# Building the one-hot gate rows of a product-key expert layer: two gated rows from one VectorE instruction in place of one from VectorE and one from GpSimd

## Chip, cores and metric

One Trainium2 chip, one of its cores. The metric is the device time in microseconds (us) of one execution of the whole program; lower is better. The engines that matter are PE (TensorE, the matmuls), DVE (VectorE), ACT (ScalarE), POOL (GpSimd) and SP (SyncE, which issues the DMAs).

## What is computed

Two blocks of a network on 256 tokens of 2048 channels in float32. The first holds a gated MLP and a stick-breaking attention, the second an mLSTM and convolution mixer and, at its end, a layer of product-key experts. Only the last is touched. Its core in the reference, cut:

```
q = (xt @ wq).reshape(-1, PEER_HEADS, 2, PEER_HALF)
s = jnp.einsum('thpc,hpnc->thpn', q, keys)
sv, si = lax.top_k(s, PEER_TOPK)                     # 16 best of 128 first keys, and of 128 second keys
...
eid = jnp.take_along_axis(cid, top_j, axis=-1)       # first key * 128 + second key: one of 16384 experts
gate = jax.nn.softmax(top_s, axis=-1)
act = jax.nn.gelu(jnp.einsum('thkd,td->thk', ue, xt))
return jnp.einsum('thk,thkd->td', gate * act, ve)
```

Each token has 8 heads with 16 experts each, so 128 pairs of keys, each with a gate.

## The kernel before

Nothing is gathered. All 16384 experts' input rows are multiplied with all tokens (the "up" loop over `u`, 32 chunks of 512 experts), the result goes through a GELU and to DRAM (`Ad`), is later multiplied with a dense matrix of gates `Gd` (zero where a token did not choose the expert), and goes into the second product with the experts' output rows.

**The matmuls.** `gemm` computes one 512-wide chunk of outputs from float32 weights that come as a stream of 1 MB tiles. Each tile is used in two halves. For a half, ACT rounds the raw weights to `wh` (line 191, from `Stream._high`), DVE makes the remainder `wl` (line 128, from `Stream._low`), and PE runs 12 matmuls of 512 columns (lines 315 to 317, in turn `wh`, `wl`, `wh`). ACT is up to six halves ahead and DVE up to five.

**The background.** Other work is written as Python generators. Between two halves `gemm` calls `bg.step()`, which takes each live generator to its next `yield`. This fixes the order of instructions on every engine when the program is built. A chunk has 8 such steps, one for each half.

**The gate matrix.** `gates_all` is such a generator and runs beside the first 16 or so chunks of the up loop. It first transposes, per token, the numbers of the first keys, of the second keys and the gates, so that tokens lie along the free axis and the 128 choices of a token on the partitions (tile `f5`: `i0`, `i1`, `gh`, `gl`). `gh` is the gate rounded to float32r and `gl` the remainder. Then, for every pair of tokens, `build` writes one-hot rows:

```
V.tensor_scalar(a[:, j, 0], C("iota"), i0[:, t:t + 1], gh[:, t:t + 1],
                op0=ALU.is_equal, op1=ALU.mult)                             # line 1181, DVE
nc.gpsimd.tensor_scalar(c[:, j], C("iota"), i1[:, t:t + 1], None, op0=ALU.is_equal)   # line 1183
nc.gpsimd.tensor_scalar(a[:, j, 1], C("iota"), i0[:, t:t + 1], gl[:, t:t + 1],
                        op0=ALU.is_equal, op1=ALU.mult)                     # line 1184, POOL
```

A matmul of `c` with both rows of `a` (line 1199, 256 columns, one for each token) gives, for one token, the 128 by 128 gates in two parts. ACT copies the one part out of PSUM, DVE adds the other (line 1204), and after 8 tokens SP sends the rows to `Gd`.

256 tokens make 128 pairs, so 128 steps, one for each half of a weight tile. A step's program: 12 weight matmuls, then two matmuls of line 1199 for pair k, then `build` for pair k+2, then the copy and the add of pair k. `a` and `c` each have three buffers in rotation (slots 0, 1, 4 and 2, 3, 5 of the tiles `e`), so the rows of pair k+3 can be written once the matmuls of pair k are done.

Of the kernel before, what the change touches and what calls it, by code (L numbers as in the profile page):

```python
# [9 lines left out]
ALU = mybir.AluOpType  # L10

P = 128
# [72 lines left out]


class Stream:
    """Weight tiles in the order of use: loaded ahead, split by halves into two float32r parts."""

    RAW, HI, LO = 3, 6, 5  # L90

# [50 lines left out]
                self._high()  # L142

    def next(self):
        """The next half, the ones before it being done with."""
        self.done = self.used
        self.ahead()
        return self.take()
# [18 lines left out]
def _block(ctx, tc, A, out):  # L167
    nc = tc.nc
# [6 lines left out]
    table = [None]  # L175
# [6 lines left out]
            table[0] = SETS[func]  # L182

    def act(out, in_, func, **kw):
        """An activation; exp and ln share the table set that holds both."""
        if func not in (AF.Copy, AF.Identity, AF.Abs, AF.Square):
            if func in SETS:
                table_for(func)
            else:
                table[0] = func  # L190
        S.activation(out, in_, func, **kw)  # L191
# [6 lines left out]
        return sb.tile([P] + shape, dt, name=nm(tag), tag=tag, bufs=bufs)  # L198

    def ft(i, shape, dt=F32):  # L200
        """A view of one of the 4 KB slots."""
        return _view(sb.tile([P, 1024], dt, name=nm(f"f{i}"), tag=f"f{i}"), shape)

    def et(i, shape, dt=F32):
        """A view of one of the 2 KB slots."""
        return _view(sb.tile([P, 512], dt, name=nm(f"e{i}"), tag=f"e{i}"), shape)

    turn = {}
# [13 lines left out]
    def ps():  # L222
        return pp.tile([P, 512], F32, name=nm("ms"), tag="ms", bufs=4)

# [1 line left out]
    order = []  # L226

    def add_w(name, n, kgs):
# [37 lines left out]
    st = Stream(nc, sb, order, act)  # L266
    bg = Background()

# [1 line left out]
    nc.scalar.preload_act_table_set("gelu_apprx_tanh_and_others")  # L270
    table[0] = AF.Gelu_apprx_tanh
    pv = tile("pv", [PW])
# [15 lines left out]
    def C(n):  # L288
        return con[:, CO[n][0]:CO[n][0] + CO[n][1]]
# [9 lines left out]

    ident = C("ident")  # L300

# [1 line left out]
    def gemm(xh, xl, kmap, evac, need={}, by_token=False):  # L303
        """One 512-wide chunk of outputs; kmap: first k tile of each stream tile;
        need: background work to end before a stream tile is used; by_token: the
        first 128 tokens end, and leave, ahead of the others."""
        acc = [pp.tile([P, 512], F32, name=nm("acc"), tag=f"acc{t}", bufs=2) for t in range(2)]
        last = len(kmap) - 1

        def mm(t, kk, wh, wl, k, first, fin):  # L310
            a = xh[:, kk, t * P:(t + 1) * P]
            b = xl[:, kk, t * P:(t + 1) * P]
            wa = wh[:, k * 512:(k + 1) * 512]
            wb = wl[:, k * 512:(k + 1) * 512]
            E.matmul(acc[t], a, wa, start=first, stop=False)  # L315
            E.matmul(acc[t], a, wb, start=False, stop=False)  # L316
            E.matmul(acc[t], b, wa, start=False, stop=fin)  # L317

        for i, k0 in enumerate(kmap):
            if by_token and i == last - 1:  # L320
                ks = [k0, k0 + 2, kmap[last], kmap[last] + 2]
                st.done = st.used
                st.ahead()
                w = [st.take() for _ in ks]
                for t in range(2):
                    for j, kk in enumerate(ks):
                        for k in range(2):
                            mm(t, kk + k, *w[j], k, i == 0 and j == 0 and k == 0, j == 3 and k == 1)
                        if t and j < 2:
                            st.release()  # L330
                        if j < 3:
                            bg.step()
                    evac(acc, t)
                    bg.step()
                return
            bg.finish(*need.get(i, []))
            for half in range(2):
                if half:
                    bg.step()
                wh, wl = st.next()  # L340
                for t in range(2):
                    for k in range(2):
                        first = i == 0 and half == 0 and k == 0
                        fin = i == last and half == 1 and k == 1
                        kk = k0 + 2 * half + k
                        mm(t, kk, wh, wl, k, first, fin)
            if i < last:
                bg.step()
        r = evac(acc)
        bg.step()  # L350
        return r
# [1 line left out]
    FULL = [0, 4, 8, 12]  # L353

    def transpose4(src, dst):
        """src(t, j) -> [128 tok, 128 ch] for 4 channel blocks; calls dst(pair, psum [128, 2, 256])."""
        for pr in range(2):
            p = ps()
            for jj in range(2):
                for t in range(2):  # L360
                    E.transpose(p[:, jj * T + t * P:jj * T + (t + 1) * P], src(t, pr * 2 + jj), ident)  # L361
            dst(pr, p)
# [10 lines left out]
        return tile(tag, [w], bufs=bufs)  # L373

    def rstd_of(dst, var, eps):
        """(var + eps) ** -0.5, a square root and a Newton step."""
        w = var.shape[-1]
        y = sm("rsy", 8, bufs=2)[:, :w]
        a = sm("rsa", 8, bufs=2)[:, :w]
        if eps is not None:  # L380
            ve = sm("rsv", 8, bufs=2)[:, :w]
            V.tensor_scalar(ve, var, eps, None, op0=ALU.add)
        else:
            ve = var
        act(y, ve, AF.Sqrt)
        V.reciprocal(y, y)
        V.scalar_tensor_tensor(a, y, -0.5, y, op0=ALU.mult, op1=ALU.mult)
        V.tensor_tensor(a, a, ve, op=ALU.mult)
        V.scalar_tensor_tensor(dst, a, 1.5, y, op0=ALU.add, op1=ALU.mult)
# [19 lines left out]
        V.scalar_tensor_tensor(d, mean, -1.0, c, op0=ALU.mult, op1=ALU.mult)  # L409
        return d  # L410

    # ================ layer 0: gated MLP with spatial gating ================
    xh = tile("xs", [NKT, T], F32R, bufs=4)
    xl = tile("xs", [NKT, T], F32R, bufs=4)
    def xprep(i, before):
# [190 lines left out]
    for n in range(4):  # L606
        out_chunk(n, 7, fin1)

    # ================ layer 1: stick-breaking attention ================
    bg.finish(p1tasks[0])  # L610
    x1h, x1l = x1["h"], x1["l"]
    r1 = x1["rstd"]
# [42 lines left out]
        V.tensor_copy(osb[g][:, :, c0:c0 + P], o[:, :256].rearrange("p (t c) -> p t c", t=2))  # L655

    def staged(gens, gap=2):
        """Chains run one stage apart, with `gap` steps of other work between the stages."""
        live = []
        while gens or live:  # L660
            for a in list(live):
                try:
                    next(a)
                except StopIteration:
                    live.remove(a)
            if gens:
                a = gens.pop(0)
                next(a)
                live.append(a)
            for _ in range(gap):  # L670
                yield
# [39 lines left out]
        gemm(x1h, x1l, FULL, ev, need)  # L711
        first = False

# [1 line left out]
    fgb = tile("phaseA", [D])  # L715
    o_ = RV["fg"][0]
    nc.sync.dma_start(out=fgb, in_=A["rows"][:, o_:o_ + D].to_broadcast([P, D]))
# [14 lines left out]
    bg.drain()  # L732

    def affine_prep(c, d, gname, bname):
        """h_res*c+d in place, then transposed with gain and bias into two parts."""
        nh = tile("xs", [NKT, T], F32R, bufs=4)
        nl = tile("xs", [NKT, T], F32R, bufs=4)

# [43 lines left out]
        return nh, nl, need  # L782

    def residual_affine(gname, bname, alloc):
        """Gain and bias on the residual itself, in the token layout."""
        gb = alloc(0)
        for n in range(4):
            g = bcast(gname, n * 512, 512, gb[:, 0:512])
# [18 lines left out]
    rstd_of(c_, ve, None)  # L807
    x2h, x2l, prep2 = affine_prep(c_, neg_prod(mean, c_), "lig", "lib")

    # ================ mLSTM and convolution mixer ================  # L810
    G5 = {}
    one = C("one")

# [223 lines left out]
        else:  # L1037
            gemm(x2h, x2l, FULL, ev)

# [1 line left out]
    st6 = new_stats(4, "st4")  # L1041
    bg.finish(*[yt5[k] for k in (("o", 0), ("o", 1), ("cB", 0))])
    for n in range(4):
# [17 lines left out]
    q7t = tile("xs", [4, 1024], bufs=4)  # L1061
    x3h, x3l, prep3 = affine_prep(*ln_scales(st6), "l1g", "l1b")

    # ================ product-key experts ================
    keysT = tile("phaseA", [16, P])
    nc.sync.dma_start(out=keysT, in_=A["keysT"])
    Gd = dr.tile([P, T, P], F32, name="Gd")
# [16 lines left out]
                yield  # L1084

    def route(n, q, before):
        """Top 16 of the products of keys for two heads; q: [128 tok, 2, 512]."""
        yield from wait(before)
        qT = ft(2, [4, T])

# [54 lines left out]
    def gates_all():  # L1145
# [27 lines left out]
        yield  # L1173

        def build(t0):
            """One-hot rows of two tokens: gates (two parts) by first key, ones by second key."""
            a = et(rot("oha", (0, 1, 4)), [2, 2, P], F32R)
            c = et(rot("ohb", (2, 3, 5)), [2, P], F32R)
            for j in range(2):
                t = t0 + j  # L1180
                V.tensor_scalar(a[:, j, 0], C("iota"), i0[:, t:t + 1], gh[:, t:t + 1],  # L1181
                                op0=ALU.is_equal, op1=ALU.mult)
                nc.gpsimd.tensor_scalar(c[:, j], C("iota"), i1[:, t:t + 1], None, op0=ALU.is_equal)  # L1183
                nc.gpsimd.tensor_scalar(a[:, j, 1], C("iota"), i0[:, t:t + 1], gl[:, t:t + 1],  # L1184
                                        op0=ALU.is_equal, op1=ALU.mult)
            return a, c

        ready = [build(0)]
# [70 lines left out]

    NP_ = NU // 2  # L1260
    def final(t):
        """Layernorm 2 of one tile of tokens, and out."""
        mv = sm("mv9", 2)
        V.bn_aggr(mv, st9[:, t])
        c = sm("cc", 1)
# [46 lines left out]


def _gate_rows(a):
    """16 rows of gates at partitions 0-7 and 32-39."""
    o = np.zeros((P,) + a.shape[1:], a.dtype)
    o[0:8], o[32:40] = a[:8], a[8:]
    return o
# [69 lines left out]
```

## Time and profile before

| | us |
|---|---|
| median of 3 runs | 3409.7 (3409.08 to 3410.12) |
| the profiled execution: span from first to last instruction | 3406.2 |
| PE busy in it | 3317.5 |
| DVE busy | 2067.0 |
| ACT busy | 1507.0 |
| POOL busy | 485.7 |
| POOL instructions of lines 1183 and 1184: first start, last start | 2054.2, 2529.2 |

The page gives the span of the profiled execution and no other time of it. The median of the runs is 3.5 us above that span. Busy times are those of one engine over the whole span; engines work beside one another, so they do not add up to it. POOL works almost only in one stretch of the program, between 2054 and 2530 us.

### The profile page before, as it was taken

The numbers are of one execution on the slowest core, as the hardware profiler recorded it, in microseconds if no ns is written. First come the engines' busy times: TensorE is split into PE (matmuls) and PEld (weight loads), VectorE is DVE, ScalarE is ACT, GpSimd is POOL, SyncE is SP. The second block draws the span as 40 slices with busy tenths as digits, with TensorE's granted clock in tenths as the row PEclk, the third lists the DMA queues.
The fourth block names the chain that finished last, engine by engine and source line by source line (L and its number), as shares of the span: only waits on it lengthen the run. The fifth ranks groups of instructions, "written<-read, shape, count | busy, mean of one in ns | idle before, by whom it ended". The sixth has DMA issues, their size and how long they took to land.

```text
span 3406.2 us, 39023 instructions
## 1 busy us (share of the span) xinstructions
PE 3317.5 (97%) x14722; PEld 2663.5 (78%) x14722; DVE 2067.0 (61%) x2966; ACT 1507.0 (44%) x1781; POOL 485.7 (14%) x522
## 2 busy tenths in 40 slices
PE   8999999999999999999999999888899999999998
PEld 6888888888888878888878887666678888888886
DVE  6565555565555566555579886555554666666666
ACT  5444444444444544444354444443344444444443
POOL 0000000000000000000000008999970000000001
PEclk9999999999999999999999999999999999999999
DMA  7565555545554445545555656555666666666664
GB/s 260 206 209 175 184 185 179 181 165 180 173 173 161 171 151 201 176 148 198 174 190 206 210 192 218 195 187 197 201 225 235 233 218 222 232 227 233 221 211 148
DMA packets 134348, 668.58 MB, mean 196 GB/s; under 512 B 12177, under 2 KB 45073, under 8 KB 62609
## 3 DMA queue, kind: packets, MB, share of 16 engines
q1 hardware_dynamic: 134160, 666.10, 56.7%
q8 instruction: 116, 1.90, 0.2%
q14 instruction: 72, 0.58, 0.0%
HBM read 630.40 MB, written 35.65 MB: 196 GB/s over the span
## 4 chain that ended last, share of the span: by engine, by line
PE 84%; POOL 14%; DVE 1%; ACT 0%; issue 0%; DMA 0%; SPq 0%; DVEq 0%; POOLq 0%
PE acc L315 27%; PE acc L316 26%; PE acc L317 26%; POOL e L1183 8%; POOL e L1184 6%; PE ms L1236 1%; PE ms L361 1%; PE ms L515 0%; DVE res L1272 0%; PE ms L1099 0%; PE ms L642 0%; PE ms L631 0%; DVE wl L128 0%; PE ms L751 0%; DMA raw<-in_aw_v_dram 0%
## 5 line engine op out<-in xcount | busy, mean ns | idle before, releaser
L128 DVE TENSOR_TENSOR wl<-raw,wh 128x1024 fp32r<-128x1024 f32 x1106 | 1343.9, 1221 | 669.4 <-PE acc L316 552.5
L191 ACT ACTIVATE wh<-raw 128x1024 fp32r<-128x1024 f32 x1106 | 1168.0, 1059 | 1198.5 <-PE acc L317 1136.3
L315 PE MATMUL acc<-wh,xs 128*128 128x512 f32 x4160 | 1662.0, 400 | 13.4 <-ACT wh L191 9.0
L316 PE MATMUL acc<-wl,xs 128*128 128x512 f32 x4160 | 1646.5, 396 | 0.5 <-DVE wl L128 0.5
L317 PE MATMUL acc<-wh,xs 128*128 128x512 f32 x4160 | 1645.9, 396 | 0.0
L315 PEld LDWEIGHTS acc<-wh,xs 128*128 128x128 f32 x4160 | 783.2, 188 | 194.2 <-ACT wh L191 9.0
L317 PEld LDWEIGHTS acc<-wh,xs 128*128 128x128 f32 x4160 | 782.6, 188 | 189.8 <-DVE xs L766 0.4
L316 PEld LDWEIGHTS acc<-wl,xs 128*128 128x128 f32 x4160 | 783.3, 188 | 178.0 <-DVE wl L128 1.0
L1183 POOL TENSOR_SCALAR e<-con,f 128x128 fp32r<-128x128 f32 x256 | 273.7, 1069 | 2053.7 <-ACT f L191 2053.7
L1184 POOL TENSOR_SCALAR e<-con,f 128x128 fp32r<-128x128 f32 x256 | 208.6, 815 | 0.0
L191 ACT ACTIVATE f<-ms 128x256 f32<-128x256 f32 (+3 forms) x153 | 62.7, 418 | 291.5 <-PE ms L1199 264.6
L1204 DVE TENSOR_TENSOR f<-ms,f 128x256 f32<-128x256 f32 x128 | 54.3, 424 | 198.1 <-ACT f L191 198.1
L1275 POOL TENSOR_TENSOR res<-res,xs 128x512 f32<-128x512 f32 x6 | 9.7, 1645 | 861.6 <-DVE res L1272 861.6
L1199 PE MATMUL ms<-e,e 128*128 128x256 f32 x256 | 82.7, 328 | 48.4 <-POOL e L1184 48.4
L1199 PEld LDWEIGHTS ms<-e,e 128*128 128x128 f32 x256 | 47.8, 187 | 92.9 <-POOL e L1184 86.5
L368 DVE TENSOR_TENSOR xs<-ms,xs 128x512 fp32r<-128x512 f32 x76 | 52.0, 690 | 110.1 <-ACT xs L191 110.1
L315 PE MATMUL acc<-wh,f 128*128 128x512 f32 x256 | 102.2, 399 | 0.0
L191 ACT ACTIVATE xs<-ms 128x512 fp32r<-128x512 f32 x76 | 44.8, 597 | 128.9 <-PE ms L1236 121.4
L316 PE MATMUL acc<-wl,f 128*128 128x512 f32 x256 | 101.2, 395 | 0.0
L317 PE MATMUL acc<-wh,f 128*128 128x512 f32 x256 | 101.2, 395 | 0.0
L1287 DVE TENSOR_TENSOR res<-res,acc 128x512 f32<-128x512 f32 x120 | 79.7, 683 | 35.1 <-PE acc L317 35.1
L1181 DVE TENSOR_SCALAR e<-con,f 128x128 fp32r<-128x128 f32 x256 | 83.4, 365 | 0.0
(213 smaller groups left out, 1355.5 us busy)
## 6 DMA issues: line engine op xcount, KB each, us to landing
raw<-in_pu_dram SPq DMA_DIRECT2D x128, 1024.0 KB, 4.9
raw<-in_pv_dram SPq DMA_DIRECT2D x128, 1024.0 KB, 4.8
raw<-in_bwi_dram SPq DMA_DIRECT2D x64, 1024.0 KB, 4.7
raw<-in_w_dram SPq DMA_DIRECT2D x56, 1024.0 KB, 4.7
raw<-in_aw_u_dram SPq DMA_DIRECT2D x32, 1024.0 KB, 4.7
raw<-in_aw_z_dram SPq DMA_DIRECT2D x32, 1024.0 KB, 4.8
raw<-in_awo_dram SPq DMA_DIRECT2D x32, 1024.0 KB, 4.7
raw<-in_aw_v_dram SPq DMA_DIRECT2D x31, 1024.0 KB, 4.8
```

The source lines that it names most:

```text
L128: self.nc.vector.tensor_tensor(l, raw[:, j * 1024:(j + 1) * 1024], self.hi[q].bitcast(F32), op=ALU.subtract)
L191: S.activation(out, in_, func, **kw)
L315: E.matmul(acc[t], a, wa, start=first, stop=False)
L316: E.matmul(acc[t], a, wb, start=False, stop=False)
L317: E.matmul(acc[t], b, wa, start=False, stop=fin)
L368: V.tensor_tensor(xl[:, k0 + 2 * pr:k0 + 2 * pr + 2, :], p.rearrange("p (k t) -> p k t", k=2), hv.bitcast(F32), op=ALU.subtract)
L1181: V.tensor_scalar(a[:, j, 0], C("iota"), i0[:, t:t + 1], gh[:, t:t + 1], op0=ALU.is_equal, op1=ALU.mult)
L1183: nc.gpsimd.tensor_scalar(c[:, j], C("iota"), i1[:, t:t + 1], None, op0=ALU.is_equal)
L1184: nc.gpsimd.tensor_scalar(a[:, j, 1], C("iota"), i0[:, t:t + 1], gl[:, t:t + 1], op0=ALU.is_equal, op1=ALU.mult)
L1199: E.matmul(p[:, j], c[:, j], a[:, j], start=True, stop=True)
L1204: V.tensor_tensor(d, p[:, :, 1], d, op=ALU.add)
L1287: V.tensor_tensor(d, d, acc[t], op=ALU.add)
```

## The change

`build` makes both gated rows of a token in one DVE instruction: a scalar_tensor_tensor that compares `iota`, repeated for two rows, with the first key, and multiplies with the two gates `gh` and `gl`, which lie side by side in `f5` (planes 2 and 3) and are each repeated along the row. POOL keeps the plain one-hot of the second key. Only docstrings and comment lines differ elsewhere; one line fewer in `build` moves later line numbers up by one (1199 is 1198 in the changed kernel, 1204 is 1203, and POOL's 1183 is 1184).

```diff
             for j in range(2):
                 t = t0 + j
-                V.tensor_scalar(a[:, j, 0], C("iota"), i0[:, t:t + 1], gh[:, t:t + 1],
-                                op0=ALU.is_equal, op1=ALU.mult)
+                V.scalar_tensor_tensor(a[:, j], C("iota")[:, None, :].to_broadcast([P, 2, P]), i0[:, t:t + 1],
+                                       f5[:, 2:4, t:t + 1].to_broadcast([P, 2, P]),
+                                       op0=ALU.is_equal, op1=ALU.mult)
                 nc.gpsimd.tensor_scalar(c[:, j], C("iota"), i1[:, t:t + 1], None, op0=ALU.is_equal)
-                nc.gpsimd.tensor_scalar(a[:, j, 1], C("iota"), i0[:, t:t + 1], gl[:, t:t + 1],
-                                        op0=ALU.is_equal, op1=ALU.mult)
             return a, c
```

How the instructions stand in their engines' queues. First POOL, at the rows of the third and fourth pair of tokens, before the change (line 1183 writes `c`, line 1184 the second row of `a`; each `e` with its two numbers is one such tile, `con` holds `iota`, `f` the transposed keys and gates; what an instruction waits for stands in brackets, DMAHW for a DMA, Pool and DVE for those engines):

```order
L1183 TENSOR_SCALAR e_760_14623<-con_71,f_748_14516 128x128 [waits DMAHW5_49,PE_49]
L1184 TENSOR_SCALAR e_759_14622<-con_71,f_748_14516 128x128 [waits DMAHW4_49]
L1183 TENSOR_SCALAR e_760_14623<-con_71,f_748_14516 128x128
L1184 TENSOR_SCALAR e_759_14622<-con_71,f_748_14516 128x128
L1183 TENSOR_SCALAR e_765_14654<-con_71,f_748_14516 128x128 [waits PE_49]
L1184 TENSOR_SCALAR e_764_14653<-con_71,f_748_14516 128x128 [waits DVE_49,Pool_49]
L1183 TENSOR_SCALAR e_765_14654<-con_71,f_748_14516 128x128
L1184 TENSOR_SCALAR e_764_14653<-con_71,f_748_14516 128x128
```

and the same place of the changed kernel, for the third to fifth pair:

```order
L1184 TENSOR_SCALAR e_760_14619<-con_71,f_748_14516 128x128 [waits DMAHW5_49,PE_49]
L1184 TENSOR_SCALAR e_760_14619<-con_71,f_748_14516 128x128
L1184 TENSOR_SCALAR e_765_14648<-con_71,f_748_14516 128x128 [waits PE_49]
L1184 TENSOR_SCALAR e_765_14648<-con_71,f_748_14516 128x128
L1184 TENSOR_SCALAR e_768_14677<-con_71,f_748_14516 128x128 [waits PE_49]
L1184 TENSOR_SCALAR e_768_14677<-con_71,f_748_14516 128x128
```

POOL has two instructions for a pair in place of four, the two that only compare; their wait on PE for the buffer stays, and the wait on DVE for the shared tile `a` is gone.

Then DVE, from the first add of line 1204 on, before the change:

```order
L1204 TENSOR_TENSOR f_757_14618<-ms_14619,f_757_14618 128x256 [waits Activation_49]
L128 TENSOR_TENSOR wl_14636<-raw_14502,wh_14596 128x1024 [waits DMAHW7_49]
L1181 TENSOR_SCALAR e_764_14653<-con_71,f_748_14516 128x128 [waits DVE_49,Pool_49]
L1181 TENSOR_SCALAR e_764_14653<-con_71,f_748_14516 128x128
L1204 TENSOR_TENSOR f_757_14618<-ms_14650,f_757_14618 128x256 [waits Activation_49]
L128 TENSOR_TENSOR wl_14665<-raw_14502,wh_14634 128x1024
```

and in the changed kernel:

```order
L1203 TENSOR_TENSOR f_757_14614<-ms_14615,f_757_14614 128x256 [waits Activation_49]
L128 TENSOR_TENSOR wl_14630<-raw_14502,wh_14592 128x1024 [waits DMAHW7_49]
L1181 SCALAR_TENSOR_TENSOR e_764_14647<-con_71,f_748_14516 128x256 [waits DVE_49]
L1181 SCALAR_TENSOR_TENSOR e_764_14647<-con_71,f_748_14516 128x256
L1203 TENSOR_TENSOR f_757_14614<-ms_14644,f_757_14614 128x256 [waits Activation_49]
L128 TENSOR_TENSOR wl_14657<-raw_14502,wh_14628 128x1024
```

The order on DVE is the same, with two instructions of 256 elements where there were two of 128, and no wait on POOL. On PE, ACT and SP no instruction is added, removed or moved.

## Rows read from the trace of the kernel before

**Rows 1.** The page's busy times of the engines.
```profile
PE 3317.5 (97%) x14722; PEld 2663.5 (78%) x14722; DVE 2067.0 (61%) x2966; ACT 1507.0 (44%) x1781; POOL 485.7 (14%) x522
```

**Rows 2.** The page's chain that ended last: by engine, then by line.
```profile
PE 84%; POOL 14%; DVE 1%; ACT 0%; issue 0%; DMA 0%; SPq 0%; DVEq 0%; POOLq 0%
PE acc L315 27%; PE acc L316 26%; PE acc L317 26%; POOL e L1183 8%; POOL e L1184 6%; PE ms L1236 1%; PE ms L361 1%; PE ms L515 0%; DVE res L1272 0%; PE ms L1099 0%; PE ms L642 0%; PE ms L631 0%; DVE wl L128 0%; PE ms L751 0%; DMA raw<-in_aw_v_dram 0%
```

**Rows 3.** Windows: length, PE, PEld, DVE, ACT, POOL busy (instructions), clock, DMA share, GB/s.
```profile
1854.00:1954.00 100.00, 100.00 (x447) 80.96 (x446) 86.07 (x222) 44.72 (x50) 0.00 (x0) 1.00 0.61 209
...
2254.00:2354.00 100.00, 89.08 (x380) 66.94 (x379) 57.45 (x109) 39.72 (x61) 100.00 (x109) 1.00 0.59 197
...
2530.00:2630.00 100.00, 99.98 (x438) 80.64 (x438) 47.86 (x44) 44.57 (x50) 0.00 (x0) 1.00 0.73 254
```

**Rows 4.** Waits between 2054 and 2530 us: total us, times, longest.
```profile
PEld ms L1199 <- POOL e L1184: 85.8, 119, 0.7
PE ms L1199 <- POOL e L1184: 48.0, 119, 0.4
```

**Rows 5.** Timeline: start, duration, engine, line; one step, and the last pair.
```profile
2200.94 0.39 PE L315 MATMUL acc<-wh,xs 128*128 128x512 f32 x1
...
2203.74 0.28 PE L1199 MATMUL ms<-e,e 128*128 128x256 f32 x1
...
2204.41 0.39 PE L1199 MATMUL ms<-e,e 128*128 128x256 f32 x1 [0.40 <-POOL e L1184]
...
2204.64 0.39 PE L315 MATMUL acc<-wh,xs 128*128 128x512 f32 x1
...
2529.34 0.28 PE L1199 MATMUL ms<-e,e 128*128 128x256 f32 x1
```

**Rows 6.** Timeline of PE, first and fifth pair of the stage.
```profile
2064.67 0.40 PE L1199 MATMUL ms<-e,e 128*128 128x256 f32 x2
...
2076.81 0.39 PE L1199 MATMUL ms<-e,e 128*128 128x256 f32 x2
```

**Rows 7.** Groups by form, 2054 to 2530 us: busy us, mean ns, idle before.
```profile
L1183 POOL TENSOR_SCALAR e<-con,f 128x128 fp32r<-128x128 f32 x256 | 273.7, 1069 | 2053.7 <-ACT f L191 2053.7
L1184 POOL TENSOR_SCALAR e<-con,f 128x128 fp32r<-128x128 f32 x256 | 208.6, 815 | 0.0
```

**Rows 8.** Groups by form of DVE, whole execution: nearest shapes to the new instruction.
```profile
L519 DVE SCALAR_TENSOR_TENSOR f<-ms,pv,f 128x256 f32<-128x256 f32 x32 | 14.0, 479 | 32.0 <-ACT f L191 18.8 <-PE ms L515 13.2
L1127 DVE TENSOR_TENSOR e<-e,f 128x256 f32<-128x256 f32 x32 | 13.6, 425 | 1.1
L419 DVE SCALAR_TENSOR_TENSOR xs<-xs,pv,xs 128x256 fp32r<-128x256 f32 x16 | 6.8, 478 | 8.2 <-ACT xs L191 8.2
```

**Rows 9.** Timeline of DVE, one step in which PE did not wait for POOL.
```profile
2071.59 0.42 DVE L1204 TENSOR_TENSOR f<-ms,f 128x256 f32<-128x256 f32 x1 [0.78 <-ACT f L191]
2071.93 1.22 DVE L128 TENSOR_TENSOR wl<-raw,wh 128x1024 fp32r<-128x1024 f32 x1
2073.07 0.60 DVE L1181 TENSOR_SCALAR e<-con,f 128x128 fp32r<-128x128 f32 x2
2074.63 0.42 DVE L1204 TENSOR_TENSOR f<-ms,f 128x256 f32<-128x256 f32 x1 [0.96 <-ACT f L191]
```

**Rows 10.** Lines 1183, 1184 (whole stage), 128 (2064 to 2530): ns minimum, median, maximum.
```profile
L1183 POOL TENSOR_SCALAR e<-con,f x256: 591/597/1646, 2054.2 to 2527.6; 128x128 fp32r<-128x128 f32 x128
L1184 POOL TENSOR_SCALAR e<-con,f x256: 787/792/1883, 2054.8 to 2529.2; 128x128 fp32r<-128x128 f32 x128
L128 DVE TENSOR_TENSOR wl<-raw,wh x127: 1215/1215/1349, 2066.2 to 2527.5; 128x1024 fp32r<-128x1024 f32 x127
```

**Rows 11.** Timeline, a POOL and a DVE instruction that meet, and POOL's next.
```profile
2068.73 0.79 POOL L1184 TENSOR_SCALAR e<-con,f 128x128 fp32r<-128x128 f32 x1
2069.51 1.21 POOL L1183 TENSOR_SCALAR e<-con,f 128x128 fp32r<-128x128 f32 x1
...
2068.90 1.35 DVE L128 TENSOR_TENSOR wl<-raw,wh 128x1024 fp32r<-128x1024 f32 x1
```

## The prediction

> **What bounds the kernel now.** I read the page first. PE is busy for 97% of the span and POOL for 14% [rows 1], which says "PE" and nothing of POOL. The chain of work that ended last says more: 84% of it is PE, but 14% lies on POOL, all on lines 1183 and 1184 [rows 2]. That is about 477 us in which the end of the program hung on GpSimd, as long as the stage in which the one-hot rows are built (2054 to 2530 us). So the windows come next: before and behind that stage PE is busy for 100 of 100 us, inside it for 89, while POOL is busy for 100 of 100 [rows 3]. The clock is 1.00 in all three, so no share of this is PE's clock. The waits inside the stage name the place: the weight load of line 1199, the one-hot matmul, waits 119 times for line 1184, 85.8 us together [rows 4].
>
> The timeline gives the size of one step. In a POOL-bound step the first weight matmul starts at 2200.94 and that of the next step at 2204.64, so 3.70 us; the pair of one-hot matmuls lies at 2203.74 and 2204.41, and the second stands until POOL's row is there [rows 5]. POOL itself needs for a pair of tokens two instructions of each line: 2 x 1069 + 2 x 815 ns = 3.77 us by the means of the stage [rows 7]; its instructions overlap by a few hundredths, hence 3.70. The stage also shows what PE needs by itself: at its start three pairs of rows are ready, and PE does not wait. Four such steps lie between 2064.67 and 2076.81, so 12.14 / 4 = 3.035 us each [rows 6]. The difference of 0.665 us, 128 steps long, is what can be had.
>
> **The change, part by part.**
>
> *POOL loses line 1184.* Per pair it keeps two comparisons. Undisturbed they take 597 ns (median), so 1.19 us a step; the stretched ones reach 1646 ns [rows 10]. The stretch comes from DVE: POOL's instruction that starts at 2069.51 takes 1.21 us and ends at 2070.72, 0.47 us after DVE's line 128 ended (2068.90 + 1.35 = 2070.25) [rows 11]. So POOL waits while DVE subtracts. One stretched and one free comparison make 1.65 + 0.60 = 2.25 us, below 3.035: POOL stops being the bound. The worst I can build is the rival below.
>
> *DVE gets a larger instruction.* The new one reads 256 elements twice from SBUF, with a scalar per partition, and writes float32r. The trace of before has no such instruction at this place, but the same kind and size elsewhere: 478 ns with both inputs in SBUF and a float32r output, 479 with one in PSUM; a plain two-input instruction of that size with repeated (broadcast) inputs takes 425 [rows 8]. I take 478, the row with the same operands; the ends are 425 and 479 before any waiting for POOL. Per step two of them take 0.96 us in place of the 0.60 that the pair takes in a step without PE waits [rows 9], so +0.36 us at most (back-to-back instructions overlap a little).
>
> *Is there room on DVE?* In such a step DVE starts the add of line 1204 at 2071.59, then line 128, then the pair until 2073.67, so 2.08 us; it stands idle for 0.96 until the next copy by ACT [rows 9]. With the change 2.08 + 0.36 = 2.44 of 3.035 us, so 0.6 us stay free. The cover is therefore this idle time; if it were gone, every further us on DVE would be a us on each step. Does a DVE busy for 2.6 us of 3.04 (86%: 0.42 + 1.22 + 0.96) hold PE up? Just ahead of the stage it is busy for 86 of 100 us with PE at 100 [rows 3]. POOL can also delay DVE: line 128 takes 1215 ns in the median and at most 1349 [rows 10], so one meeting cost up to 0.134 us; two a step make 0.27 and 2.71 us, still inside.
>
> *Moved waits.* DVE's instruction no longer waits for POOL, as both writers of tile `a` are now one. Behind it on DVE stands the add of line 1204, and behind that line 128, which is made up to five halves ahead of PE. The rows of a pair are written two steps before their matmul, and POOL may run up to three buffers ahead, so a late comparison or a late product has a step and more before PE sees it. ACT's copy is released by the matmul as before; ACT is at 40% in the stage [rows 3]. A GELU pair at a chunk's end (some 16 in the stage) may come ahead of that copy and make it late; it was so before as well, and DVE's idle time takes it.
>
> *DMA.* No transfer is added or moved, but the stage's transfers come in less time: 197 GB/s x 3.70 / 3.035 = 240 GB/s. Behind the stage 254 GB/s flow with PE at 99.98 of 100 us [rows 3]; I cost this at nothing.
>
> *The sum.* From the first one-hot matmul (2064.67) to that of the last pair (2529.34) [rows 5, 6] are 464.67 us for 127 steps. At 3.035 us they take 385.4, so 79.2 less; the last pair's own wait adds 0.67. Together 79.9 us. The waits count gives about the same: 119 times 0.665 is 79.1. Nothing else on the chain changes, since the stages around it keep PE at 100%. The profiled execution has a span of 3406.2 us and would have 3326.3; the median of the runs lies 3.5 us above that span, and I add the same. **3409.7 - 79.9 = 3329.8, say 3330 us.** Upwards, if a meeting on DVE at its largest (0.134 us) reached PE in a third of the steps, 43 x 0.134 = 6 us: 3336. Downwards nothing, as PE's own steps are the floor: 3329.
>
> **The rivals.**
>
> *POOL stays the bound, at a lower level.* The new instruction has two SBUF inputs, like line 128, and should stop POOL in the same way; line 1181 of before had one. If at every step the one comparison meets line 128 (1.65 us, the maximum) and the other the whole pair of new ones (0.60 + 0.96 = 1.56), POOL needs 3.20 us: 127 x 3.20 = 406.4 in place of 464.7, 58 to 59 us less with the last wait: 3351. For it: the stretch is in the trace at every step. Against it: DVE's 0.6 us of idle time a step let one comparison start undisturbed, and a POOL instruction that has started before DVE's runs on at its usual length (790 ns for the one of 2068.73, although DVE began 0.17 us later [rows 11]). Chance 0.10, spread over 3336 to 3351.
>
> *DVE becomes the bound, held by POOL for whole instructions.* If each comparison stopped DVE for its full 597 ns, DVE would need 2.44 + 1.19 = 3.63 us a step, 127 x 3.63 = 461.0: 4 us gained, 3405. With some of them falling into DVE's idle time or beside the add, which has one input in PSUM, the step is that of the two-input work and POOL alone, 1.22 + 0.96 + 1.19 = 3.37, 428 us: 3373. Against it: in the one meeting of this kind DVE was 0.13 us late, where the rest of POOL's instruction was 0.62 [rows 10, 11]. Chance 0.04. The Trainium skill has this as its rule (SBUF — State Buffer, section "Who interferes with whom"): a VectorE instruction with two SBUF inputs and a GpSimd one that reads SBUF exclude each other, the first to start keeps the shared port for the whole instruction, and the other stands still. By that rule the change would cost DVE what GpSimd gains. The trace agrees for POOL behind DVE, and not for DVE behind POOL.
>
> *Slower.* The same hold, but without the overlap of instructions that follow one another on DVE, which a stop in each of them would take away: then the busy times simply add up, 0.42 + 1.22 + 0.96 + 1.19 = 3.79 us a step, above the 3.70 of now. 127 x 3.79 = 481.3, 17 us more: 3426. It decides from the point at which DVE and POOL together need over 3.66 us (464.7 / 127), so from about 0.6 us of hold per comparison, four times the largest seen. Chance 0.02.
>
> *No gain, because another wait sits behind POOL's.* PE could find `wl` late, or the PSUM copy. Its steps at 3.035 us ran with DVE at 2.08 us of them, not with 2.44, so this is not shown. The loss would have no natural size; I put it anywhere between 3336 and 3410. Chance 0.02.
>
> **How the numbers follow.** The forecast, PE-bound steps throughout, has 0.82 and lies between 3329 and 3336. The range starts a us below that for the spread of the runs and takes in the nearer half of the first rival: 3328 to 3344. What a measurement of this kernel can tell from no change is about 0.2%, 7 us. Faster by more: the forecast, the first rival, most of the second and half of the fourth, 0.96. Within it: 0.02, the far ends of the second and fourth. Slower: 0.02.
>
> **What would show it.** In the profile after, PE should be at 99 or 100 of 100 us in the stage and the stage about 80 us shorter (some 390 us from the first to the last one-hot matmul); the wait of PE for POOL at the one-hot matmul gone; POOL's share of the chain gone; POOL busy for some 2 us a step; line 1181 at 256 elements and 0.48 us (up to 0.6 where it meets POOL); DVE idle for about 0.6 us a step before the add. I am wrong on POOL if its busy share in the stage is still 100 of 100; wrong on DVE if line 1181 takes 0.8 us or more, or line 128 well over 1.35, with PE waiting for DVE.

## Result and the profile after

| | before | after |
|---|---|---|
| median of 4 runs, us | 3409.85 (3409.08 to 3410.12) | 3328.47 (3327.70 to 3328.76) |
| span of the profiled execution, us | 3406.2 | 3327.0 |
| POOL busy, us | 485.7 | 162.9 |
| DVE busy, us | 2067.0 | 2107.4 |

The ratio of the runs is 0.9762, 95% interval 0.9748 to 0.9776: 81 us less. The forecast was 3330, the range 3328 to 3344. One of all the executions below, in the run with nothing on POOL, took 7159.67 us and is left out.

The page's busy times and its chain by engine, of the changed kernel, beside [rows 1, 2]:

```profile
PE 3286.7 (99%) x14722; PEld 2663.8 (80%) x14722; DVE 2107.4 (63%) x2966; ACT 1505.1 (45%) x1781; POOL 162.9 (5%) x266
...
PE 98%; DVE 1%; ACT 0%; DMA 0%; issue 0%; SPq 0%; DVEq 0%
```

POOL, 14% of the chain before, is gone from it. The windows of the changed kernel (length, then busy time of PE, PEld, DVE, ACT and POOL with instructions, clock, DMA share, GB/s), the first inside the stage and the second behind it, beside [rows 3]:

```profile
2254.00:2354.00 100.00, 100.00 (x464) 81.63 (x463) 80.63 (x132) 48.30 (x74) 39.02 (x66) 1.00 0.73 241
...
2450.00:2550.00 100.00, 100.00 (x440) 80.67 (x439) 48.06 (x45) 44.57 (x50) 0.00 (x0) 1.00 0.74 259
```

PE is at 100 of 100 us where it was at 89, and DMA moves 241 GB/s with no wait of PE. The waits of the stage (waiter, releaser: us in total, times, longest) have turned round: no engine waits for POOL, and POOL waits for PE, beside [rows 4]:

```profile
POOL e L1184 <- PE ms L1198: 235.3, 125, 5.8
ACT f L191 <- PE ms L1198: 184.6, 111, 1.7
DVE f L1203 <- ACT f L191: 76.9, 127, 1.9
```

The length of the stage is the first and the last start of the one-hot matmuls. In this view of the tile `e` stand the duration's minimum, median and maximum in ns, then the first and last start. First the kernel before:

```profile
L1199 PE MATMUL ms<-e,e x256: 275/281/388, 2064.7 to 2530.0; 128*128 128x256 f32 x128
```

and the changed one:

```profile
L1198 PE MATMUL ms<-e,e x256: 275/281/284, 2065.6 to 2450.9; 128*128 128x256 f32 x128
```

465.3 us became 385.3: 80.0 us are won here, and the longest matmul no longer holds a wait (388 ns before). The two spans differ by 79.2; the stage began 0.9 us later in this execution, in a part of the program that the change does not touch.

One step of the changed kernel on DVE, in the timeline (start, duration, what ended the idle time before), beside [rows 9], then POOL in the same step:

```profile
2202.92 0.42 DVE L1203 TENSOR_TENSOR f<-ms,f 128x256 f32<-128x256 f32 x1 [0.58 <-ACT f L191]
2203.27 1.32 DVE L128 TENSOR_TENSOR wl<-raw,wh 128x1024 fp32r<-128x1024 f32 x1
2204.51 0.87 DVE L1181 SCALAR_TENSOR_TENSOR e<-con,f 128x256 fp32r<-128x256 f32 x2
2205.96 0.42 DVE L1203 TENSOR_TENSOR f<-ms,f 128x256 f32<-128x256 f32 x1 [0.58 <-ACT f L191]
...
2202.57 1.18 POOL L1184 TENSOR_SCALAR e<-con,f 128x128 fp32r<-128x128 f32 x2 [1.85 <-PE ms L1198]
```

The step is 3.04 us (2202.92 to 2205.96). DVE stands idle for 0.58 of it, and POOL works for 1.18 and waits for 1.85. Both work beside PE with room to spare.

### The profile page after: what moved, and what is told of

Its sections match the earlier page's. It is cut to its first block, busy times and chain, and to the rows that moved or that the text cites. A ratio compares the mean times of both kernels' runs of the same rounds, so it can differ in the third digit from the quotient of the medians.

```text
span 3327.0 us, 38516 instructions
## 1 busy us (share of the span) xinstructions
PE 3286.7 (99%) x14722; PEld 2663.8 (80%) x14722; DVE 2107.4 (63%) x2966; ACT 1505.1 (45%) x1781; POOL 162.9 (5%) x266
## 4 chain that ended last, share of the span: by engine, by line
PE 98%; DVE 1%; ACT 0%; DMA 0%; issue 0%; SPq 0%; DVEq 0%
PE acc L315 31%; PE acc L316 31%; PE acc L317 31%; PE ms L1198 1%; PE ms L1235 1%; PE ms L361 1%; PE ms L515 0%; DVE res L1271 0%; PE ms L751 0%; PE ms L1099 0%; PE ms L642 0%; PE ms L631 0%; DVE wl L128 0%; DMA raw<-in_aw_v_dram 0%; ACT xs L191 0%; PE ms L898 0%
## 5 line engine op out<-in xcount | busy, mean ns | idle before, releaser
L1184 POOL TENSOR_SCALAR e<-con,f 128x128 fp32r<-128x128 f32 x256 | 153.0, 610 | 2289.9 <-ACT f L191 2054.6
L1181 DVE SCALAR_TENSOR_TENSOR e<-con,f 128x256 fp32r<-128x256 f32 x256 | 111.4, 474 | 0.0
L1286 DVE TENSOR_TENSOR res<-res,acc 128x512 f32<-128x512 f32 x120 | 79.7, 683 | 35.1 <-PE acc L317 35.1
L191 ACT ACTIVATE f<-acc 128x512 f32<-128x512 f32 x84 | 49.8, 598 | 38.0 <-PE acc L317 36.6
L539 DVE TENSOR_TENSOR res<-res,acc 128x512 f32<-128x512 f32 x64 | 43.7, 686 | 30.8 <-PE acc L317 30.8
L317 PEld LDWEIGHTS acc<-wh,f 128*128 128x128 f32 x256 | 48.1, 188 | 11.6
```

The costliest lines, as they stand in the source:

```text
L539: V.tensor_tensor(d, d, acc[t], op=ALU.add)
L1181: V.scalar_tensor_tensor(a[:, j], C("iota")[:, None, :].to_broadcast([P, 2, P]), i0[:, t:t + 1], f5[:, 2:4, t:t + 1].to_broadcast([P, 2, P ...
L1286: V.tensor_tensor(d, d, acc[t], op=ALU.add)
```

## Experiments

**Theory A**: a step takes the longest of three times, PE's 3.035 us, POOL's and DVE's. Before, POOL's was the longest (3.70); the change takes line 1184 from POOL, and PE's is left. **Theory B**: the gain came from the form of the new instruction (one for two), or from the end of the tile that two engines wrote.

### Both rows on DVE in the old form

```diff
-                V.scalar_tensor_tensor(a[:, j], ... i0[:, t:t + 1], ... op0=ALU.is_equal, op1=ALU.mult)
+                V.tensor_scalar(a[:, j, 0], C("iota"), i0[:, t:t + 1], gh[:, t:t + 1], ...)
+                V.tensor_scalar(a[:, j, 1], C("iota"), i0[:, t:t + 1], gl[:, t:t + 1], ...)
```

> Edit: both gated rows on DVE, but as two instructions of 128 elements per token (the old form), POOL keeps the plain row. Theory A (the step is the longest of PE's 3.035 us, POOL's time and DVE's time; the gain came from POOL's second line leaving POOL): POOL needs 1.19 us a step, DVE 0.34 + 1.24 + 4 x 0.30 to 0.34 = 2.8 to 2.95 us, both under 3.035, so the time is that of the changed kernel, 3328 to 3331 us, PE never waits for POOL. Theory B (the gain came from the fused instruction, which removes work on DVE or the shared writing of one tile by two engines): four instructions on DVE lose a part of it, 3345 us or more.

Measured: 3328.29 us, ratio to before 0.9759 (0.9743 to 0.9775), as the changed kernel. DVE's add now stands idle 0.34 us a step in place of 0.58:

```profile
2303.25 0.34 DVE L1183 TENSOR_SCALAR e<-con,f 128x128 fp32r<-128x128 f32 x1
2303.93 0.42 DVE L1204 TENSOR_TENSOR f<-ms,f 128x256 f32<-128x256 f32 x1 [0.34 <-ACT f L191]
```

So fusing the two rows saves DVE about 0.24 us a step, and the program nothing. The first half of theory B falls: without the new instruction the gain is the same.

### All gated rows on POOL

```diff
-                V.scalar_tensor_tensor(a[:, j], ... op0=ALU.is_equal, op1=ALU.mult)
+                nc.gpsimd.tensor_scalar(a[:, j, 0], C("iota"), i0[:, t:t + 1], gh[:, t:t + 1], ...)
+                nc.gpsimd.tensor_scalar(a[:, j, 1], C("iota"), i0[:, t:t + 1], gl[:, t:t + 1], ...)
```

> Edit: the opposite way, both gated rows on POOL, none on DVE. No tile is written by two engines any more. Theory A: POOL's step grows from 3.70 us by two instructions of 0.79 us to 5.28 us, so 127 x (5.28 - 3.035) = 285 us over the changed kernel, 3613 us (3600 to 3640). Theory B (two engines writing one tile was the cost): not slower than the kernel before, 3410 us or less.

Measured: 3583.44 us (one run), below the expected 3600 to 3640. No tile has two writers here, and the time is 173 us over before, which is not what theory B expects. The step is 5.05 us, not 5.28 as expected: POOL's timeline has the comparison that meets line 128 at 1.38 us where it was 1.57 in the kernel before, since it had started 0.30 us after line 128 (2302.33) and not 0.11:

```profile
2301.86 0.79 POOL L1183 TENSOR_SCALAR e<-con,f 128x128 fp32r<-128x128 f32 x1
2302.63 1.38 POOL L1185 TENSOR_SCALAR e<-con,f 128x128 fp32r<-128x128 f32 x1
2304.00 0.79 POOL L1181 TENSOR_SCALAR e<-con,f 128x128 fp32r<-128x128 f32 x1
```

### The row goes on being made on POOL, for nobody

```diff
+        scr = tile("scr", [2, P], F32R)
...
+                nc.gpsimd.tensor_scalar(scr[:, 0], C("iota"), i0[:, t:t + 1], gl[:, t:t + 1], ...)
```

> Edit: the changed kernel, and POOL still makes its old gated row of each token, into a scratch tile that nobody reads. Theory A: POOL's instructions are in order, so the plain row of the next token stands behind the useless one and POOL is the bound again: 3.70 us a step or, as the new DVE instruction stops POOL too, up to 3.70 + 0.96 = 4.66 us: 3413 to 3535 us. Theory B (what mattered is who waits for the row, not POOL's time): 3328 to 3335 us.

Measured: 3438.23 us (one run), 28 us slower than before. So POOL's time counts, whoever reads the row. PE waits again, and POOL's means show what the new DVE instruction adds. The useless row (line 1187) takes 1394 ns in the mean and the plain row (line 1186) 614, together 2008. Before, the same two took 815 and 1069 [rows 7], together 1884. So the standing has moved from the plain row to the other, and a pair of tokens costs POOL 0.25 us more:

```profile
L1187 POOL TENSOR_SCALAR scr<-con,f 128x128 fp32r<-128x128 f32 x198 | 275.9, 1394 | 0.0
...
L1186 POOL TENSOR_SCALAR e<-con,f 128x128 fp32r<-128x128 f32 x198 | 121.5, 614 | 0.0
```

The step is 3.94 us in the timeline, 0.24 more than the 3.70 of before. The two longer DVE instructions would have made the kernel slower if POOL had kept its work.

### Half the change

```diff
+                if j == 0:
                     V.scalar_tensor_tensor(a[:, j], ... op0=ALU.is_equal, op1=ALU.mult)
+                else:
+                    V.tensor_scalar(a[:, j, 0], C("iota"), i0[:, t:t + 1], gh[:, t:t + 1], ...)
+                    nc.gpsimd.tensor_scalar(a[:, j, 1], C("iota"), i0[:, t:t + 1], gl[:, t:t + 1], ...)
```

> Edit: half the change: of each pair the first token's gated rows come from the new DVE instruction, the second token's as before (one row by DVE, one by POOL). Theory A: POOL needs 2 x 0.60 + 0.79 + about 0.97 of standing behind line 128 = 2.95 us a step, just under 3.035, so nearly the whole gain: 3328 to 3335 us; if POOL also stands for one new instruction (0.47 us) in each step, 3.4 us and 3375 us. A theory in which the gain goes in proportion to the rows moved: half of it, 3369 us.

Measured: 3329.39 us, ratio 0.9764 (0.9748 to 0.9781): the whole gain for half of the rows. There is a threshold, not a proportion. The tile `a` still has two writers here, for the second token, and PE does not wait, so the second half of theory B falls too. The window is the best lesson of the study:

```profile
2254.00:2354.00 100.00, 100.00 (x463) 81.65 (x462) 74.35 (x133) 48.28 (x75) 100.00 (x100) 1.00 0.72 241
```

POOL is "busy" for 100 of 100 us, as before the change, yet PE is too, and nobody waits for POOL. Its timeline tells why, with DVE's below it:

```profile
2299.96 1.88 POOL L1188 TENSOR_SCALAR e<-con,f 128x128 fp32r<-128x128 f32 x1
2301.83 1.18 POOL L1190 TENSOR_SCALAR e<-con,f 128x128 fp32r<-128x128 f32 x2
2303.00 1.88 POOL L1188 TENSOR_SCALAR e<-con,f 128x128 fp32r<-128x128 f32 x1
...
2302.74 1.22 DVE L128 TENSOR_TENSOR wl<-raw,wh 128x1024 fp32r<-128x1024 f32 x1
2303.87 0.50 DVE L1182 SCALAR_TENSOR_TENSOR e<-con,f 128x256 fp32r<-128x256 f32 x1
```

The gated row takes 1.88 us, 1.09 more than its 0.79 alone [rows 10]; this much of POOL's busy time is standing behind DVE. It began 0.26 us after line 128 and ended 0.51 us after the new instruction that follows line 128 (2304.88 and 2304.37), so it stood behind both. A step of POOL takes 3.04 us, as PE's does. That the meeting with DVE shifts until POOL's step fits PE's is a reading of this timeline, and no run tests it.

### Nothing on POOL

```diff
-                nc.gpsimd.tensor_scalar(c[:, j], C("iota"), i1[:, t:t + 1], None, op0=ALU.is_equal)
+                V.tensor_scalar(c[:, j], C("iota"), i1[:, t:t + 1], None, op0=ALU.is_equal)
```

> Edit: the changed kernel with the plain row on DVE as well, so POOL has nothing to do in the stage. DVE then needs 0.34 + 1.13 (line 128 without POOL beside it) + 2 x 0.40 + 2 x 0.30 to 0.34 = 2.9 to 2.95 us a step. Theory A: still under PE's 3.035, so 3328 to 3333 us, line 128 back at 1215 ns. Rival (DVE has less room than the idle time says, because it must follow ACT's copy in each step): DVE sets the step, 3.1 to 3.25 us, 3337 to 3356 us, PE waits for DVE.

Measured: 3328.41 to 3330.40 us in three executions, ratio 0.9767 (0.9747 to 0.9786): no difference from the changed kernel that this can tell. DVE has 0.29 us idle left, and works for 90 of 100 us:

```profile
2302.70 0.42 DVE L1203 TENSOR_TENSOR f<-ms,f 128x256 f32<-128x256 f32 x1 [0.29 <-ACT f L191]
```

Line 128 is back at a median of 1215 ns; beside POOL it was 1323. A plain comparison costs DVE 280 ns when POOL is silent.

### One and two more of the new instruction

Into the scratch tile of above, one more per pair (with `if j == 0:`), and two more (for each token):

```diff
+                V.scalar_tensor_tensor(scr, C("iota")..., i0[:, t:t + 1], f5[:, 2:4, t:t + 1]..., ...)
```

> Edit: the changed kernel with one more of the new DVE instructions per pair of tokens, into a scratch tile. DVE's idle time of 0.58 us a step takes its 0.40 us. Theory A: 3328 to 3331 us. Rival (the idle time is no room): 0.40 us x 127 = 50 us more, 3379 us.

Measured: 3328.12 us, ratio 0.9761 (0.9741 to 0.9780): the idle time is real room.

> Edit: as the one before, with two more of them per pair: 0.79 us where 0.58 are free. Theory A: DVE becomes the bound at 3.17 to 3.25 us a step, 17 to 27 us over the changed kernel: 3345 to 3356 us, PE waits for DVE in the stage. Rival (buffers ahead of PE hide it): 3328 us.

Measured: 3334.49 us, ratio 0.9779 (0.9760 to 0.9799), 6 us over the changed kernel: past the point, as theory A says, but by less than the 17 to 27 us expected. Both executions (3333.39 and 3335.60) lie above all of the changed kernel (3328.76 at most). DVE is at 100 of 100 us and its add no longer waits:

```profile
2302.12 0.41 DVE L1208 TENSOR_TENSOR f<-ms,f 128x256 f32<-128x256 f32 x1
2302.46 1.21 DVE L128 TENSOR_TENSOR wl<-raw,wh 128x1024 fp32r<-128x1024 f32 x1
2303.59 0.51 DVE L1183 SCALAR_TENSOR_TENSOR e<-con,f 128x256 fp32r<-128x256 f32 x1
...
2305.24 0.41 DVE L1208 TENSOR_TENSOR f<-ms,f 128x256 f32<-128x256 f32 x1
```

The step is 3.12 us here (2302.12 to 2305.24), which over 127 steps would be 11 us. The windows show why it is less:

```profile
2154.00:2254.00 100.00, 100.00 (x463) 81.62 (x462) 100.00 (x195) 48.20 (x75) 65.79 (x67) 1.00 0.72 231
2254.00:2354.00 100.00, 100.00 (x452) 79.71 (x451) 100.00 (x194) 47.32 (x72) 79.23 (x65) 1.00 0.72 232
```

DVE is the slower one in both, but PE starts 463 matmuls in the first, as in the changed kernel, and 452 in the second. By the starts of the one-hot matmuls the first 66 steps take 3.03 us each and the other 61 take 3.12 in the mean. That adds 5 us, and the stage is 390.4 us in place of 385.3. DVE falls behind by 0.085 us a step from the start, and PE feels it once 66 x 0.085 = 5.6 us are used up, a little less than the two steps by which the rows are made ahead. PE's busy share is 100 in both windows, so the share does not show this wait; the count of matmuls does.

### Only the high part of the gates

Here the low part of every gate is left out: no subtraction for it, a gated row of 128 elements, a one-hot matmul of 128 columns, no add.

```diff
-                V.scalar_tensor_tensor(a[:, j], ...)
+                V.tensor_scalar(a[:, j], C("iota"), i0[:, t:t + 1], gh[:, t:t + 1], ...)
...
-                    E.matmul(p[:, j], c[:, j], a[:, j], start=True, stop=True)
+                    E.matmul(p[:, j, 0], c[:, j], a[:, j], start=True, stop=True)
...
-                V.tensor_tensor(d, p[:, :, 1], d, op=ALU.add)
```

> Edit: the changed kernel without the low part of the gates: it is not computed, the gated row is one instruction of 128 elements, the one-hot matmul has 128 columns in place of 256, and the add on DVE is gone. This leaves out the low part of every gate. Theory A (after the change the stage stands on PE's own instructions and on nothing else): PE's pair of matmuls takes 0.12 us in place of 0.235, so a step of 2.92 us and 128 x 0.117 = 15 us less: 3313 us (3311 to 3316). Rival (something else, DVE, POOL or a wait of the changed kernel, sets the step): 3325 us or more.

Measured: 3328.61 us, ratio 0.9763 (0.9747 to 0.9779): nothing gained, against theory A's 15 us. The time is the rival's (3325 or more), but its reason is not there: no wait of PE is listed, and DVE stands idle for 1.2 us a step, in half of the steps until PE releases a buffer (63 times, 78.2 us). The one-hot matmuls give the stage:

```profile
L1196 PE MATMUL ms<-e,e x256: 221/247/273, 2066.9 to 2451.4; 128*128 128x128 f32 x128
```

These 384.5 us over 127 steps are 3.03 us each, where 2.92 were expected. PE's timeline shows where the columns went. In this kernel:

```profile
2303.01 0.33 PE L1196 MATMUL ms<-e,e 128*128 128x128 f32 x2
2303.18 0.45 PE L315 MATMUL acc<-wh,xs 128*128 128x512 f32 x1
2303.47 0.40 PE L316 MATMUL acc<-wl,xs 128*128 128x512 f32 x1
```

and in the changed kernel, with 256 columns:

```profile
2302.18 0.39 PE L1198 MATMUL ms<-e,e 128*128 128x256 f32 x2
2302.41 0.40 PE L315 MATMUL acc<-wh,xs 128*128 128x512 f32 x1
2302.64 0.39 PE L316 MATMUL acc<-wl,xs 128*128 128x512 f32 x1
```

From the pair to line 316 it is 0.46 us in both: what the pair saves (0.17 for 0.23) line 315 gives back (0.29 for 0.23). The weight loads of this kernel,

```profile
2302.78 0.42 PEld L1196 LDWEIGHTS ms<-e,e 128*128 128x128 f32 x2
2303.12 0.19 PEld L315 LDWEIGHTS acc<-wh,xs 128*128 128x128 f32 x1
2303.24 0.19 PEld L316 LDWEIGHTS acc<-wl,xs 128*128 128x128 f32 x1
```

and of the changed kernel

```profile
2304.98 0.42 PEld L1198 LDWEIGHTS ms<-e,e 128*128 128x128 f32 x2
2305.32 0.19 PEld L315 LDWEIGHTS acc<-wh,xs 128*128 128x128 f32 x1
2305.44 0.19 PEld L316 LDWEIGHTS acc<-wl,xs 128*128 128x128 f32 x1
```

follow one another at the same distances (0.34, 0.12). This fits a pair whose price is that of its weight loads and not of its columns; no run with other weight loads tests it. So the stage stands on PE, as theory A has it, but narrowing this matmul to 128 columns did not shorten PE's own time. A version faster than the changed kernel did not come out of the study.

### How long POOL holds DVE

One POOL instruction per pair in place of two, of 256 elements and then of 512. Both rows get the first token's key, so the second token's own second key is left out.

```diff
-                nc.gpsimd.tensor_scalar(c[:, j], C("iota"), i1[:, t:t + 1], None, op0=ALU.is_equal)
+            nc.gpsimd.tensor_scalar(c, C("iota")[:, None, :].to_broadcast([P, 2, P]), i1[:, t0:t0 + 1], None, ...)
```

> Edit: the changed kernel, but POOL writes the plain rows of a pair in one instruction of 256 elements, both with the first token's key (so the second token's own key is left out). It starts with the release by PE, about 0.70 us ahead of line 128, and takes 0.9 to 1.2 us. If POOL keeps a two-input DVE instruction out until it ends: line 128 is stretched by 0.2 to 0.5 us, to 1.4 to 1.7. If the hold is short (about 0.11 us, at the instruction's beginning): line 128 at 1215 ns. Time 3327 to 3330 us either way, as DVE has 0.58 us to spare.

> Edit: as the one before with 512 elements (the further two rows are written and not read), some 1.7 to 2.2 us of POOL. If POOL keeps DVE out until it ends: line 128 is stretched by 1.0 to 1.5 us, DVE's step passes 3.035 us by 0.4 to 0.9 us and the time grows to 3380 to 3440 us. If the hold is short: line 128 at 1215 to 1350 ns, 3327 to 3331 us. If the two take turns by the element: line 128 and POOL's instruction both stretched by a part of that.

Measured: 3327.88 and 3327.32 us (one run each). Line 128 has a median of 1215 ns in the first and 1216 in the second. The timeline of the second, POOL and then DVE:

```profile
2301.28 1.56 POOL L1184 TENSOR_SCALAR e<-con,f 128x512 fp32r<-128x512 f32 x1 [1.47 <-PE ms L1199]
...
2301.91 1.22 DVE L128 TENSOR_TENSOR wl<-raw,wh 128x1024 fp32r<-128x1024 f32 x1
```

DVE started 0.63 us into an instruction that ran for another 0.93 us, and neither was stretched. POOL therefore does not keep DVE out until it ends. But in the same run line 128 takes up to 1474 ns, where DVE came earlier. Again POOL, then DVE:

```profile
2140.85 1.57 POOL L1184 TENSOR_SCALAR e<-con,f 128x512 fp32r<-128x512 f32 x1 [1.80 <-PE ms L1199]
...
2141.14 1.47 DVE L128 TENSOR_TENSOR wl<-raw,wh 128x1024 fp32r<-128x1024 f32 x1
```

DVE started 0.29 us into POOL's instruction and lost 0.255 us (1.47 for 1.215). Start and loss together say that it was let in about 0.55 us after POOL's start. Another meeting gives the same (0.33 us in, 1.44 us, at 2335.28). In the changed kernel, where line 128 starts 0.11 us after the second comparison began (2202.57 + 0.59 = 2203.16, and 2203.27), it is stretched by 0.11 (1323 for 1215): let in after 0.22 us. With 256 elements it is 0.34 (0.29 us in, 1.26 us, at 2141.73). So by these few meetings the hold lies at the beginning of POOL's instruction and grows with its elements: 0.22, 0.34 and 0.55 us for 128, 256 and 512, each time a little over a third of the instruction's 0.59, 0.92 and 1.57 us. At most steps of the two runs DVE came after it (0.63 us in), which is why the medians show nothing. To be first by a little is not enough: in the run with one more instruction, line 128 began 0.07 us into a comparison (2295.71 and 2295.64), took its 1.22 us, and POOL stood, 1.67 us for 0.60.

### The kernel before, once more

> The kernel before once more, with a profile. In the paired runs the gain is 81 to 82 us, the sum of the prediction 79.9. If the profile that the sum was made from was of an execution that happened to be about 2 us shorter than most, this one's span is 3408 to 3409 us, and the 2 us are found in one place of it: in the one-hot stage (then its step is a little over 3.70 us, up to 3.715) or outside of it (then they are no part of the change).

Measured: 3408.82 us, span 3407.0. The one-hot matmuls:

```profile
L1199 PE MATMUL ms<-e,e x256: 275/280/388, 2065.5 to 2530.9; 128*128 128x256 f32 x128
```

465.4 us, as in the first profile. The expected 3408 to 3409 us of span was not met, and the stage is not longer either. From this execution to the profiled one of the changed kernel the spans differ by 80.0 us, the same as the stage.

## Why the prediction was right

- **The bound and the floor.** PE's step without waits, 3.035 us from four steps at the start of the stage [rows 6], held for all of it: 385.3 us / 127 = 3.03. This was the step that carried the sum.
- **The sum.** 79.9 us forecast, 80.0 in the stage. The medians differ by 81.4. The prediction took 3.5 us between span and median; this was two things, about 1.8 us around a span (3408.82 for 3407.0 in the repeated run) and a profiled execution shorter than most. Where the last 1.4 us of the 81.4 lie stays open: two profiles of before agree on the stage to 0.1 us, so it is not seen there, and single executions of that kernel differ by more than this (3407.18 to 3410.49 us).
- **The new instruction.** 478 ns taken, 474 measured (median), the pair 0.87 us where 0.96 was the upper price. The row with the same operands elsewhere in the program [rows 8] was the right one.
- **Room on DVE.** 0.6 us forecast, 0.58 measured, and the runs with one and two more instructions put the limit where this says. Line 128 is stretched by 0.11 us at most steps, inside the 0.134 taken from the largest meeting of before [rows 10]. This bound was the largest meeting that had happened, and not the most that a POOL instruction can cost: a comparison of 512 elements cost DVE 0.255 us. The window called "just ahead of the stage" (86 of 100 us on DVE) ends 100 us before it; in the last 100 us DVE is at 84, which serves as well.
- **POOL.** The direction was right, the size not: 2.25 us a step, one comparison stretched, was forecast, and it is 1.18 with none. The prediction let POOL meet line 128 as before; freed from being the bound, it starts when PE releases a buffer, 0.70 us ahead of line 128 (2202.57 and 2203.27), and starts both comparisons before DVE reads.
- **The sign it named for POOL was not a good one.** "Wrong on POOL if its busy share is still 100 of 100": half the change has just that, and the whole gain. The stage of "some 390 us" named beside it does not follow from the sum, which has 385.4.
- **The rivals.** POOL as a bound at a lower level did not come, for the reason given above. Where POOL keeps its work, as in the run with the useless row, the new instruction does stop it: 3.94 us a step. The rival that DVE is held for whole instructions falls by the run with 512 elements, where it was held for the first 0.55 of 1.57 us. The Trainium skill's rule (SBUF — State Buffer, section "Who interferes with whom"), that the first to start keeps the port for its whole instruction, holds in these traces for POOL behind DVE (1.88 us for 0.79 in the half change) and not for DVE behind POOL (1.22 us of line 128 beside 0.93 us of a running POOL instruction, and 1.47 us, not the 2.5 of a hold to the end, when it came 0.29 us in); here the measurement decides.

## What to carry to other kernels

Where PE waits for a helper once in each step of a pipelined stage, compare the step's length with PE's own, read from steps in which the helper was ahead; the difference times the steps is the gain, and it is had in full as soon as the helper's time falls below PE's, here with half of the work moved. Before moving work to another engine, read that engine's idle time per step and price the instruction by a row with the same kinds of operands; here 0.4 us more per step was free and 0.8 was not. A busy share of 100% says nothing by itself, since it counts the time that an engine stands behind another.

## What the runs showed of the hardware that was not expected

- GpSimd's busy time holds its waiting for a two-input VectorE instruction: 1.88 us for an instruction of 0.79, and a full 100 of 100 us without being the bound.
- The hold the other way covers only the beginning of the GpSimd instruction and grows with its elements: VectorE's two-input subtraction was let in 0.22, 0.34 and 0.55 us after the start of comparisons of 128, 256 and 512 elements, which run for 0.59, 0.92 and 1.57 us.
- VectorE's comparison of 128 elements (one scalar) took 280 ns with GpSimd silent.
- A one-hot matmul pair of 128 columns moved the next matmuls no earlier than one of 256; the weight loads kept their distances.
- TensorE's busy share stays at 100 of 100 us while it is held up by 0.085 us a step (two more of the new instruction); it starts 452 matmuls there in place of 463.
- With all gated rows on POOL, PE worked for 76 of 100 us, with a mean granted clock of 0.87 to 0.89 in those windows (1.00 in all others shown here), so some of it at the lower level; since PE waited for POOL there, this cost nothing that the step of 5.05 us shows.
